# The output products of both feed-forward networks by Strassen's scheme, with the sums of products made in PSUM

## The chip, the cores and the metric

One core of a Trainium2 chip runs the whole kernel. The metric is device time in microseconds (us), shorter is better; three runs of the kernel before gave a median of 3192.24 us. TensorE is called PE, VectorE DVE, ScalarE ACT, GpSimd POOL, and SP is the engine that only issues transfers.

## What is computed

A decoder block: 16 meta tokens are put in front of 1024 tokens, and each of two half-step feed-forward networks (FFN1 before the mixing layers, FFN2 after them) does

```
gate, up = split(rmsnorm(h) @ w_gu, 2)         # 1024 -> 2 x 2816
h = h + 0.5 * (silu(gate) * up) @ w_down       # 2816 -> 1024
```

Between them stand a gated DeltaNet and an RWKV-7 branch, which the change doesn't touch. Everything is float32. The change is to the second product, `@ w_down`, of both networks. Its inner size 2816 is 22 tiles of 128 features, its output 1024 is 8 tiles.

## The kernel before

Features lie on the 128 partitions and tokens along the free axis. A float32 operand x is split into two parts, hi = x rounded to the matmul type, copied by ACT, and lo = x - hi, subtracted by DVE or, where an engine is named, by POOL (`split`). A product then is three matmuls for each tile of inner features: hi by hi, hi by lo, lo by hi (`mm3`, L250 to L260).

`gate_up` (L404) makes silu(gate) * up. It already uses Strassen's scheme in Winograd's form, with 7 products of half-sized quarters instead of 8: the 1040 (FFN1) or 1024 (FFN2) tokens are cut into two halves, the inner features into two halves, the output features into two halves. Its products go to PSUM one by one and DVE adds them up in SBUF (L428). Its results go to DRAM as 22 tiles `hid` (L476).

`down` (L518) is the second product. It takes the 22 tiles of `hid` in four groups of 6, 6, 5 and 5 (`GROUPS`). `Hidden` loads them back (`hr`, three buffers) and splits them (`hd`, eight buffers). Within a group it goes over the 8 output tiles m; for each, `loadw` hands out the weight tile `w` (raw `wraw` by DMA, split by ACT and DVE, one tile ahead), PE makes all matmuls of the group for one chunk of tokens into one PSUM tile `pd`, and DVE adds half of it to the residual `h` (L539). So each weight is split once for a group and used for all tokens, and each `pd` is read once. In the last group the chunks of tokens come one after the other, so that each half of h is done as early as possible: FFN1 then stores it, sums its squares and builds the inputs `uk` of the next stage (`after_block`, L605 to L621); FFN2 makes the final norm and stores the output (L674 to L695). The residual is loaded again from DRAM on POOL's queue when `down` begins (L586, L671). At that point `gate_up` is making its last products and storing the last tiles of `hid`.

A scheduler sets the order of each engine's instructions at build time from the program's data dependences and the buffers of each pool; at run time every engine works through its own list in that order, and an instruction whose inputs or buffer aren't there holds up all behind it on its engine. A tile of a pool with one buffer can be written again only when the last reader of the earlier tile is done.

Of the kernel before, what the change touches and what calls it, by code (L numbers as in the profile page):

```python
# [8 lines left out]
F32 = mybir.dt.float32  # L9
F32R = mybir.dt.float32r  # L10
AF = mybir.ActivationFunctionType
ALU = mybir.AluOpType
# [9 lines left out]
GROUPS = [6, 6, 5, 5]  # L22
# [166 lines left out]
def weight_order():  # L189

    def down_order(n):
        f = 0
        for G in GROUPS:
            for _ in range(2 if f + G == NF else 1):
                for m in range(KD):
                    yield f"wdn{n}", (m, slice(None), slice(f, f + G)), G
            f += G

    def tiles(cts, j=0):
        for ct in cts:  # L200
            yield "win", (ct + j % NJ,), KD

    yield from down_order(1)
    for act, it in schedule():
        yield from tiles(USES.get(act, ()), 0 if act == "segment" else it)
    for _ in range(2):
        for m in range(KD):
            yield "wout", (m,), KD

    yield None  # L210
    yield from down_order(2)
# [51 lines left out]
class Rms:  # L263


    def __init__(self, g, sq, n, add_on=None):
        self.g, self.sq, self.n, self.acc, self.k = g, sq, n, None, 0
        self.eng = add_on or g.nc.vector
# [213 lines left out]
class Hidden:  # L482

    AHEAD = 3

    def __init__(self, g, pool, tot):
        self.g, self.pool, self.tot, self.raws, self.first = g, pool, tot, [], None

    def load(self, f):
        raw = self.pool.tile([P, self.tot], F32, name="hr", tag="hr", bufs=self.AHEAD)  # L490
        self.g.nc.sync.dma_start(raw, self.g.hid[f][:, : self.tot])
        self.raws.append(raw)

    def put(self, hd):
        raw = self.raws.pop(0)
        split(self.g, raw, hd[:, 0, :], hd[:, 1, :])
        return hd

    def ahead(self):
        for f in range(self.AHEAD):  # L500
            self.load(f)
        yield
        yield
        fetchw(self.g)
        yield
        yield
        self.first = self.put(self.pool.tile([P, 2, self.tot], F32R, name="hd0", tag="hd0"))
        yield
        yield


    def tiles(self, sp, f0, G, bufs):
        hid = []
        for f in range(f0, f0 + G):
            if f >= self.AHEAD:
                self.load(f)
            hid.append(self.put(sp.tile([P, 2, self.tot], F32R, name="hd", tag="hd", bufs=bufs)) if f else self.first)
        return hid  # L518


def down(g, sp, hs, which, chunks, hooks, hidden, bufs):

    nc = g.nc
    f0 = 0
    for G in GROUPS:
        hid = hidden.tiles(sp, f0, G, bufs)
        last = f0 + G == NF
        if last:
            hooks.before_last()
        for ci, cs in enumerate([[c] for c in chunks] if last else [chunks]):  # L530
            for m in range(KD):
                wd = loadw(g, f"wdn{which}", m, slice(None), slice(f0, f0 + G))
                for t0, n in cs:
                    pd = mm_tile(g, "pd", n)
                    for c0, cn in halves(n):
                        sl = slice(t0 + c0, t0 + c0 + cn)
                        mm3(g, pd[:, c0 : c0 + cn], wd, G, lambda k: (hid[k][:, 0, sl], hid[k][:, 1, sl]))
                    hv = hs[m][:, t0 : t0 + n]
                    nc.vector.scalar_tensor_tensor(hv, pd, 0.5, hv, op0=ALU.mult, op1=ALU.add)  # L539
                if last:  # L540
                    hooks.after_block(ci, m)
        f0 += G


def ffn1(g):
    tc, nc = g.tc, g.nc
    n = T // 2
    with ExitStack() as ctx:
# [29 lines left out]
        hidden = Hidden(g, ctx.enter_context(tc.tile_pool(name="f1d", bufs=1, reuse_waits="tile")), T)  # L578
# [3 lines left out]
        xctx = ExitStack()  # L582
        sp = ctx.enter_context(tc.tile_pool(name="f1", bufs=1, reuse_waits="tile"))
        hs = [sp.tile([P, T], F32, name=f"h{k}") for k in range(KD)]
        for k in range(KD):
            nc.gpsimd.dma_start(hs[k], g.a["hT"][k])  # L586
        hooks = K()
# [36 lines left out]
        down(g, sp, hs, 1, [c[:2] for c in SEGS], hooks, hidden, 8)  # L624
# [3 lines left out]
def ffn2(g):  # L628
# [3 lines left out]
    with ExitStack() as ctx:  # L632
        right = ExitStack()
        bp = ctx.enter_context(tc.tile_pool(name="f2b", bufs=1, reuse_waits="tile"))
        b = {x: bp.tile([P, HK, 2, n], F32R, name=f"b{x}") for x in ("11", "21")}
# [27 lines left out]
        hidden = Hidden(g, ctx.enter_context(tc.tile_pool(name="f2d", bufs=1, reuse_waits="tile")), SEQ)  # L663
        with tc.tile_pool(name="gs", bufs=1, reuse_waits="tile") as sp:
            gu.send((hidden.ahead(), sp))
        right.close()
        sp = ctx.enter_context(tc.tile_pool(name="f2", bufs=1, reuse_waits="tile"))
        hs = [sp.tile([P, SEQ], F32, name=f"hh{k}") for k in range(KD)]
        for s in range(2):
            for k in range(KD):  # L670
                nc.gpsimd.dma_start(hs[k][:, s * n : (s + 1) * n], g.h3dr[k] if s else g.h2dr[k])  # L671
        hooks = K()
        hooks.before_last = lambda: None
        big = lambda name: sp.tile([P, 4, n], F32, name=name, tag="hd", bufs=8)  # L674
# [23 lines left out]
        down(g, sp, hs, 2, [(0, n), (n, n)], hooks, hidden, 8)  # L698
# [825 lines left out]
```

## Time and profile before

| what | value |
|---|---|
| median of 3 runs | 3192.24 us (3190.23 to 3200.6) |
| the profiled execution's own time | 3192.63 us |
| its span (first to last instruction) | 3190.9 us |
| mean granted TensorE clock | 0.982 |
| PE busy | 3047.0 us, 95% of the span |
| DVE, ACT, POOL busy | 1950.3, 1320.5, 540.7 us |
| FFN1's output product | 497.1 to 761.4 us |
| FFN2's output product | 2925.5 to 3177.4 us |

The profile counts an engine as busy while it has an instruction under way. For PE the ends of matmuls are modelled and overlap, so what counts is how many matmuls start in a stretch. "Idle before, releaser" names what ended an engine's wait. The granted clock is the share of full speed that PE was allowed. Line numbers are those of the kernel before.

### The profile page before, as it was taken

How to read it: one execution, taken by the hardware profiler on the slowest of the kernel's cores; microseconds unless marked ns; L12 is line 12 of the kernel's file. 1: busy time of each engine (PE TensorE's matmuls, PEld its weight loads, DVE VectorE, ACT ScalarE, POOL GpSimd, SP SyncE). 2: the span in 40 equal slices, each digit the busy share in tenths (PEclk: the TensorE clock that was granted, in tenths of full speed). 3: DMA queues.
4: the chain of work that ended last, by engine and by line, in shares of the span. 5: the costliest groups of instructions: out<-in, count | busy, mean ns of one | idle time of the engine just before them, and what ended most of it. 6: DMA issues, size and time to landing. Idle time of an engine off the chain costs nothing. (4 is left out here: it accounts for less than half of the span.)

```text
span 3190.9 us, 57986 instructions
## 1 busy us (share of the span) xinstructions
PE 3047.0 (95%) x23606; PEld 2526.7 (79%) x23606; DVE 1950.3 (61%) x3820; ACT 1320.5 (41%) x2260; POOL 540.7 (17%) x810
## 2 busy tenths in 40 slices
PE   5999999999999999999999999999999899999998
PEld 5999998998877877787776777777776688887886
DVE  7555544346676676676767777777766755555335
ACT  4222222125555545464565455545544422222114
POOL 4222220000011011111111111111101433222000
PEclk8999999999999999999999999999999999999999
DMA  2322224234222222222333232233344232224323
GB/s 93 97 91 80 80 84 160 77 96 141 60 67 75 71 71 58 75 75 69 96 84 78 69 79 72 70 82 76 104 133 172 67 102 86 80 81 149 106 79 111
DMA packets 256554, 286.93 MB, mean 90 GB/s; under 512 B 168272, under 2 KB 174416, under 8 KB 256288
## 3 DMA queue, kind: packets, MB, share of 16 engines
q1 hardware_dynamic: 252048, 271.42, 28.8%
q0 software_dynamic: 2512, 8.65, 0.7%
q8 instruction: 185, 3.03, 0.4%
q10 hardware_dynamic: 1728, 3.16, 0.3%
q14 instruction: 81, 0.66, 0.1%
HBM read 232.70 MB, written 50.47 MB: 89 GB/s over the span
## 5 line engine op out<-in xcount | busy, mean ns | idle before, releaser
L259 PE MATMUL pp<-uk,w 128*128 128x264 f32 (+1 forms) x4824 | 981.0, 353 | 8.1 <-DVE gg L1410 4.5
L259 PEld LDWEIGHTS pp<-uk,w 128*128 128x128 f32 x4824 | 750.3, 192 | 129.7 <-issue 20.3
L154 ACT ACTIVATE w<-wraw 128x1024 fp32r<-128x1024 f32 (+2 forms) x332 | 328.6, 990 | 707.5 <-PE pd L259 288.9
L259 PE MATMUL pd<-hd,w 128*128 128x512 f32 (+1 forms) x2640 | 499.7, 351 | 13.8 <-DVE w L155 6.7
L259 PEld LDWEIGHTS pd<-hd,w 128*128 128x128 f32 x2640 | 428.9, 190 | 83.3 <-DVE w L155 8.6
L422 PE MATMUL pg<-bt,w 128*128 128x260 f32 (+1 forms) x2772 | 457.5, 322 | 22.4 <-ACT bt L154 8.9
L422 PEld LDWEIGHTS pg<-bt,w 128*128 128x128 f32 x2772 | 401.2, 190 | 67.3 <-ACT bt L154 9.6
L428 DVE TENSOR_TENSOR c<-c,pg 128x520 f32<-128x520 f32 (+1 forms) x308 | 208.2, 689 | 368.2 <-PE pg L422 303.4
L155 DVE TENSOR_TENSOR w<-wraw,w 128x1024 fp32r<-128x1024 f32 (+2 forms) x332 | 382.5, 1152 | 63.9 <-ACT w L154 58.4
L422 PE MATMUL pg<-b,w 128*128 128x260 f32 (+1 forms) x2376 | 391.3, 321 | 10.5 <-POOL b L155 5.0
L422 PEld LDWEIGHTS pg<-b,w 128*128 128x128 f32 x2376 | 344.9, 190 | 45.6 <-POOL b L155 5.4
L392 POOL TENSOR_TENSOR wrx<-wrx 128x512 f32<-128x512 f32 x44 | 66.6, 1514 | 575.2 <-DVE w22b L155 305.7
L154 ACT ACTIVATE w<-wrx 128x1024 fp32r<-128x1024 f32 (+1 forms) x66 | 60.2, 912 | 184.9 <-PE pg L422 173.3
L1357 POOL TENSOR_SCALAR sgam<-SBn,gam 128x64 f32<-128x64 f32 x112 | 63.1, 563 | 432.0 <-DVE SBn L1371 400.5
L1230 DVE TENSOR_TENSOR Xb<-Xb,tb 115x126 f32<-115x126 f32 (+22 forms) x496 | 126.7, 255 | 11.3
L1228 DVE TENSOR_TENSOR tb<-Ub,Xb 115x126 f32<-115x126 f32 (+22 forms) x496 | 125.6, 253 | 10.7
L1039 DVE SCALAR_TENSOR_TENSOR acc<-xr,pk,acc 128x528 f32<-128x528 f32 (+1 forms) x144 | 109.0, 757 | 37.5 <-ACT acc L1035 35.0
L539 DVE SCALAR_TENSOR_TENSOR h<-pd,h 128x528 f32<-128x528 f32 (+1 forms) x64 | 44.6, 698 | 119.8 <-PE pd L259 119.8
L539 DVE SCALAR_TENSOR_TENSOR hh<-pd,hh 128x512 f32<-128x512 f32 x64 | 44.2, 690 | 108.4 <-PE pd L259 105.9
L259 PE MATMUL pwo<-uk,w 128*128 128x512 f32 x384 | 104.1, 414 | 5.6 <-DVE w L155 2.1
L1371 DVE SCALAR_TENSOR_TENSOR SBn<-b,gam,sgam 128x64 f32<-128x64 f32 x128 | 36.2, 283 | 94.3 <-PE b L1354 93.9
L835 ACT ACTIVATE sh<-pp,pk 128x528 f32<-128x528 f32 (+1 forms) x54 | 37.3, 691 | 130.7 <-PE pp L259 111.1
(373 smaller groups left out, 4104.9 us busy)
## 6 DMA issues: line engine op xcount, KB each, us to landing
wraw<-in_win SPq DMA_DIRECT2D x150, 512.0 KB, 3.5
wraw<-in_wgu SPq DMA_DIRECT2D x44, 512.0 KB, 3.4
wrx<-in_wgu SPq DMA_DIRECT2D x44, 512.0 KB, 3.5
wraw<-in_wdn SPq DMA_DIRECT2D x48, 320.0 KB, 2.9
wraw<-in_wdn SPq DMA_DIRECT2D x32, 384.0 KB, 3.1
hid<-c SPq DMA_DIRECT2D x44, 260.0 KB, 4.0
hr<-hid SPq DMA_DIRECT2D x22, 520.0 KB, 9.8
hid<-c SPq DMA_DIRECT2D x44, 256.0 KB, 3.1
```

The lines of the kernel that those rows point to most:

```text
L154: g.nc.scalar.activation(hi, src, AF.Copy)
L155: (eng or g.nc.vector).tensor_tensor(lo, src, hi.bitcast(F32), op=ALU.subtract)
L259: g.nc.tensor.matmul(ps, lhsT=l, rhs=r, start=i == 0, stop=i == n - 1)
L392: nc.gpsimd.tensor_tensor(a22, a21, a22, op=ALU.add)
L422: nc.tensor.matmul(ps[:, c0 : c0 + cn], lhsT=l[:, x, k, :], rhs=r[:, k, y, c0 : c0 + cn], start=i == 0, stop=i == 3 * HK - 1)
L428: nc.vector.tensor_tensor(o, x, y, op=ALU.add)
L539: nc.vector.scalar_tensor_tensor(hv, pd, 0.5, hv, op0=ALU.mult, op1=ALU.add)
L835: nc.scalar.activation(sh[:, 1 : 1 + n], ps, AF.Identity, scale=g.V("mu", i))
L1039: nc.vector.scalar_tensor_tensor(acc[:, :n], xr[:, tap : tap + n], V("convw", ct * 4 + tap), acc[:, :n], op0=ALU.mult, op1=ALU.add)
L1228: nc.vector.tensor_tensor(tv, U[:, i, i + 1 :].unsqueeze(2).to_broadcast([npt, nt, ncc]), X[:, i, 0:ncc].unsqueeze(1).to_broadcast([npt, n ...
L1230: nc.vector.tensor_tensor(X[:, i + 1 :, 0:ncc], X[:, i + 1 :, 0:ncc], tv, op=ALU.add)
L1357: nc.gpsimd.tensor_scalar(sg, SB, gam, None, op0=ALU.mult)
```

## The change

The output product takes 18 of the 22 tiles of `hid` by the same scheme of 7 products, in three groups (`NSG`) of six tiles: quarters of three tiles (`GP`) by half of the tokens. The remaining four tiles (`FREST` to `NF`) go as before, chunk after chunk. There are 12 units of work in each network: group by group, and within a group four pairs of output tiles, m and m + 4.

What is added for each unit: two raw weight tiles (`wraw`, `wrc`) and from them six weight forms. "11" and "12" are split as they are (tile `w`). POOL then makes four sums in place in the raw tiles, for the forms "s3" and "s1" (tile `wd31`) and "s2" and "s4" (tile `wd24`). The form "22" (tile `wd22`, the only one with one buffer) is split before those sums, since the first of them writes over a22. What is added for each group: seven forms of the hidden tiles (`down_forms`: 11, t1, t2, 21, t3, 22, t4), again with sums in place, and one buffer for each form. What replaces the sums on DVE: products that share a term are accumulated in the same PSUM tile, with an add to the residual after each step; the three PSUM tiles of a unit are x, y and z, and y gathers four of the seven products.

The program asks for the seven products of a unit in this order, here numbered as they are spoken of below: y1 = 11 by 11, z1 = s1 by t1, y2 = s2 by t2, x = 12 by 21, y3 = s3 by t3, z2 = s4 by 22, y4 = 22 by t4. The first number is the weight form, the second the hidden form. In FFN1 a product is 18 matmuls of 260 columns, in FFN2 9 of 512.

```diff
+GP = 3
+NSG = 3
+FREST = 2 * GP * NSG
...
+def down_weights(g, which, grp, m):
...
+    a = g.wp.tile([P, KD, P], F32, name="wraw", tag="wraw", bufs=2)[:, : 2 * GP]
+    nc.sync.dma_start(a, g.a[f"wdn{which}"][m, :, fs])
+    put(g.wp.tile([P, 2, KD, P], F32R, name="w", tag="w", bufs=WB), a, "11", "12")
+    yield w
+    new = lambda name, k: g.wd.tile([P, 2, k, P], F32R, name=name, tag=name, bufs=2 if k > GP else 1)
+    c = g.wd.tile([P, 2 * GP, P], F32, name="wrc", tag="wrc", bufs=2)
+    nc.sync.dma_start(c, g.a[f"wdn{which}"][m + HK, :, fs])
+    a11, a12, a21, a22 = a[:, :GP], a[:, GP:], c[:, :GP], c[:, GP:]
+    put(new("wd22", GP), a22, "22", eng=nc.gpsimd)
+    nc.gpsimd.tensor_tensor(a22, a21, a22, op=ALU.add)
+    nc.gpsimd.tensor_tensor(a21, a11, a21, op=ALU.subtract)
+    put(new("wd31", 2 * GP), c, "s3", "s1")
+    nc.gpsimd.tensor_tensor(a11, a22, a11, op=ALU.subtract)
+    nc.gpsimd.tensor_tensor(a12, a12, a11, op=ALU.subtract)
+    put(new("wd24", 2 * GP), a, "s2", "s4")
+    yield
...
+def down_forms(g, hidden, grp, place):
...
+    if grp:
+        put("11", b11)
+    else:
+        b["11"] = hidden.b11
+    sums(nc.gpsimd, b11, b12, b11)
+    put("t1", b11)
+    sums(nc.vector, b11, b22, b11)
+    put("t2", b11)
+    put("21", b21, nc.gpsimd)
+    sums(nc.vector, b12, b22, b12)
+    put("t3", b12)
+    put("22", b22, nc.gpsimd)
+    sums(nc.gpsimd, b21, b21, b11)
+    put("t4", b21)
...
+def down(g, hs, which, chunks, hooks, hidden, place, wctx):
...
+    for i, (grp, m) in enumerate(units):
+        l = w
+        if i + 1 < len(units):
+            nxt = down_weights(g, which, *units[i + 1])
+            w = next(nxt)
+            next(nxt)
...
+        x, y, z = (mm_tile(g, name, n) for name in ("pdx", "pdy", "pdz"))
+
+        product(y, l["11"], b["11"], stop=False)
+        add(h11, y)
+        product(z, l["s1"], b["t1"], stop=False)
+        add(h22, z)
+        product(y, l["s2"], b["t2"], False, False)
+        add(h12, y)
+        product(x, l["12"], b["21"])
+        add(h11, x)
+        product(y, l["s3"], b["t3"], False, False)
+        add(h22, y)
+        product(z, l["s4"], b["22"], False)
+        add(h12, z)
+        product(y, l["22"], b["t4"], False)
+        add(h21, y)
+        if m == HK - 1:
+            if grp + 1 < NSG:
+                b = down_forms(g, hidden, grp + 1, place)
...
+    for ci, (t0, n) in enumerate(chunks):
+        for m in range(KD):
+            wd = loadw(g, f"wdn{which}", m, slice(None), slice(FREST, NF))
...
-        for s in range(2):
-            for k in range(KD):
+        for k in (0, 4, 1, 5, 2, 6, 3, 7):
+            for s in range(2):
                 nc.gpsimd.dma_start(hs[k][:, s * n : (s + 1) * n], g.h3dr[k] if s else g.h2dr[k])
```

On PE, in the middle of FFN1's output product: before, the matmuls of one output tile go through the hidden tiles `hd` with one weight tile `w`, three at a time.

```order
L259 MATMUL pd_5070<-hd_4951,w_4966 128x512 x3
L259 MATMUL pd_5070<-hd_4956,w_4966 128x512 x3
L259 MATMUL pd_5070<-hd_4961,w_4966 128x512 x3
L259 MATMUL pd_5095<-hd0_4880,w_5029 128x264 x3
L259 MATMUL pd_5095<-hd_4943,w_5029 128x264 x3
```

Now, on PE, this is one whole unit, the third of FFN1's first group (`hd0`, `ht1`, `h21` and so on are hidden forms, `w`, `wd31`, `wd24`, `wd22` weight forms):

```order
L589 MATMUL pdy_5376<-hd0_4884,w_5201 128x260 x18
L589 MATMUL pdz_5377<-ht1_4980,wd31_5211 128x260 x2
L589 MATMUL pdx_5375<-h21_4997,w_5201 128x260 x6
L589 MATMUL pdy_5376<-ht2_4990,wd24_5216 128x260 x2
L589 MATMUL pdz_5377<-ht1_4980,wd31_5211 128x260 x16
L589 MATMUL pdy_5376<-ht2_4990,wd24_5216 128x260 x16
L589 MATMUL pdx_5375<-h21_4997,w_5201 128x260 x12
L589 MATMUL pdy_5376<-ht3_5007,wd31_5211 128x260 x18
L589 MATMUL pdz_5377<-h22_5014,wd24_5216 128x260 x18
L589 MATMUL pdy_5376<-ht4_5024,wd22_5206 128x260 x18
```

What moved: one weight tile for each output tile has become four for each pair, the second, third and fourth product are broken up and mixed, and `wd22` is read last.

On ACT, at the same place, with what each row waits for: before, one copy for each weight tile.

```order
L154 ACTIVATE w_5218<-wraw_5216 128x768 [waits DMAHW2_49,DVE_49,PE_49]
L154 ACTIVATE w_5281<-wraw_5279 128x768 [waits DMAHW3_49,DVE_49,PE_49]
L154 ACTIVATE w_5344<-wraw_5342 128x768 [waits DMAHW4_49,DVE_49,PE_49]
L154 ACTIVATE w_5407<-wraw_5405 128x768 [waits DMAHW5_49,DVE_49,PE_49]
L154 ACTIVATE hd_5485<-hr_5483 128x1040 [waits DMAHW6_49,PE_49]
```

Now, on ACT, the copies for the unit shown above and the first two of the next one:

```order
L157 ACTIVATE wd22_5206<-wrc_5204 128x384 [waits DMAHW2_49,PE_49,Activation_49]
L157 ACTIVATE wd31_5211<-wrc_5204 128x768 [waits Pool_49]
L157 ACTIVATE wd24_5216<-wraw_5199 128x768 [waits Pool_49]
L157 ACTIVATE w_5513<-wraw_5511 128x768 [waits DMAHW5_49,DVE_49,PE_49]
L157 ACTIVATE wd22_5362<-wrc_5360 128x384 [waits DMAHW2_49,PE_49,Activation_49]
L157 ACTIVATE wd31_5367<-wrc_5360 128x768 [waits DVE_49,Pool_49]
```

What moved: the copies for a unit now wait for POOL, and that into `wd22` for PE. The PE instruction waited for is the last matmul that reads the earlier `wd22`, the last of y4 of the unit before.

On DVE, where FFN1's second group begins (`ht3`, `ht4` are the new group's hidden forms; L555 a sum in place, L582 an add to the residual, `pdy_5761` the y of the new group's first unit):

```order
L555 TENSOR_TENSOR hr_5035<-hr_5041,hr_5035 128x520
L158 TENSOR_TENSOR ht3_5704<-hr_5031,ht3_5704 128x520
L158 TENSOR_TENSOR ht3_5704<-hr_5033,ht3_5704 128x520
L158 TENSOR_TENSOR wd31_5523<-wrc_5516,wd31_5523 128x768
L158 TENSOR_TENSOR ht3_5704<-hr_5035,ht3_5704 128x520
L158 TENSOR_TENSOR wd24_5528<-wraw_5511,wd24_5528 128x768
L158 TENSOR_TENSOR w_5742<-wraw_5740,w_5742 128x768
L158 TENSOR_TENSOR ht4_5721<-hr_5037,ht4_5721 128x520
L158 TENSOR_TENSOR ht4_5721<-hr_5039,ht4_5721 128x520
L158 TENSOR_TENSOR ht4_5721<-hr_5041,ht4_5721 128x520
L582 SCALAR_TENSOR_TENSOR h0_4944<-pdy_5761,h0_4944 128x520
L582 SCALAR_TENSOR_TENSOR h4_4946<-pdz_5762,h4_4946 128x520
```

Before, on DVE between the first two groups (`hd` are the new group's hidden tiles, `h0` its first add):

```order
L539 SCALAR_TENSOR_TENSOR h7_4934<-pd_5410,h7_4934 128x528
L155 TENSOR_TENSOR hd_5485<-hr_5483,hd_5485 128x1040
L155 TENSOR_TENSOR hd_5490<-hr_5488,hd_5490 128x1040
L539 SCALAR_TENSOR_TENSOR h7_4934<-pd_5448,h7_4934 128x512
L155 TENSOR_TENSOR hd_5495<-hr_5493,hd_5495 128x1040
L155 TENSOR_TENSOR w_5500<-wraw_5498,w_5500 128x768
L155 TENSOR_TENSOR hd_6004<-hr_6002,hd_6004 128x1040
L539 SCALAR_TENSOR_TENSOR h0_4927<-pd_5503,h0_4927 128x528
```

What moved: the first add of a new group stands behind all seven forms of that group and three weight splits; before, it stood behind four of the group's splits. On POOL, the loads of the residual (L586 and L671, now issued tile by tile in the order 0, 4, 1, 5, ...) now stand ahead of the splits of `h21` and `h22` and the sums for `ht4` of each network's first unit.

155 lines of the change are left out of this document (96 added, 59 removed).

## The prediction

> **What bounds the kernel now.** The page's first part says that PE is busy nearly all the time. What counts is its pace in the two stretches of the output product, which the table by stage gives, asked for parts well inside them (the first two rows), inside `gate_up` (the third) and for the whole stretches:
>
> ```profile
> PE 3047.0 (95%) x23606; PEld 2526.7 (79%) x23606; DVE 1950.3 (61%) x3820; ACT 1320.5 (41%) x2260; POOL 540.7 (17%) x810
> ```
>
> ```profile
> 530.00:700.00 170.00, 170.00 (x1076) 154.39 (x1076) 60.90 (x74) 27.98 (x32) 0.00 (x0) 1.00 0.26 78
> 2955.00:3140.00 185.00, 185.00 (x818) 153.21 (x817) 75.61 (x95) 39.17 (x48) 0.00 (x0) 1.00 0.28 85
> 100.00:200.00 100.00, 100.00 (x837) 100.00 (x836) 53.19 (x68) 26.85 (x34) 25.79 (x20) 1.00 0.31 100
> 497.10:761.40 264.30, 257.39 (x1591) 232.23 (x1590) 124.21 (x159) 67.76 (x87) 9.14 (x19) 0.98 0.38 125
> 2925.50:3177.40 251.90, 244.50 (x1063) 198.52 (x1062) 118.30 (x148) 66.66 (x83) 11.74 (x18) 1.00 0.37 118
> ```
>
> The columns are the stretch, its length, then busy time and number of instructions of PE, weight load, DVE, ACT and POOL, the granted clock and the transfers. PE never waits in the first three: 0.158 us for a matmul in FFN1's product (two of 264 columns to one of 512), 0.226 us for one of 512 in FFN2's, 0.1195 us for one of 260. DVE, ACT and POOL have time to spare. In the last two rows, the whole stretches, PE's own work is 1584 x 0.158 = 250.3 and 1056 x 0.226 = 238.8 us, so 14.0 and 13.1 us are lost today, most of it at the start. So fewer matmuls are worth their full time, as long as PE goes on without waiting.
>
> **What is saved.** FFN1: 12 units of 126 matmuls of 260 columns, 1512 x 0.1195 = 180.7 us, and the last four tiles with 288 x 0.158 = 45.5; together 226.2, saved 24.1 us. FFN2: 756 + 192 = 948 matmuls of 512, 214.4 us, saved 24.4. In all 48.5 us, if PE never waits more than today.
>
> **The wait in each unit.** By the rows of ACT's order the copy into `wd22` waits for PE's last matmul of the unit before, because `wd22` has one buffer. Behind that copy hangs a chain: POOL's lo of "22", the sum into a22, the difference into a21, ACT's copy into `wd31`, and only then z1, the second product. PE has y1 alone to bridge it. The prices, from the groups by line and from the order of time in `gate_up`, where the same operations stand with 512 columns:
>
> ```profile
> L154 ACT ACTIVATE w<-wraw 128x768 fp32r<-128x768 f32 x16 | 13.5, 846 | 94.0 <-PE pd L259 82.3 <-issue 9.4 <-PE pg L422 2.3
> L154 ACT ACTIVATE w22b<-wrx 128x512 fp32r<-128x512 f32 x11 | 6.8, 619 | 0.9 <-DMA wrx<-in_wgu 0.8
> L393 POOL TENSOR_TENSOR wrx<-wraw,wrx 128x512 f32<-128x512 f32 x19 | 24.4, 1287 | 1.5
> 434.46 1.29 POOL L394 TENSOR_TENSOR wraw<-wrx,wraw 128x512 f32<-128x512 f32 x1
> 435.83 1.29 POOL L395 TENSOR_TENSOR wraw<-wraw 128x512 f32<-128x512 f32 x1
> 437.16 1.06 ACT L154 ACTIVATE w<-wraw 128x1024 fp32r<-128x1024 f32 x1 [7.27 <-POOL wraw L395]
> 462.75 0.64 PE L422 MATMUL pg<-b,w 128*128 128x260 f32 x4
> 462.88 1.06 ACT L154 ACTIVATE w<-wrx 128x1024 fp32r<-128x1024 f32 x1 [4.67 <-PE pg L422]
> ```
>
> Handing over takes 0.13 us from PE to ACT (462.75 to 462.88) and 0.04 between the others (435.83 + 1.29 to 437.16). ACT's copy of 384 columns is 0.50 us by the slope from 512 to 768. POOL's operation of 384 columns is not in the trace; three quarters of 1.29 is 0.97, with something fixed in it 1.0, and one follows the other by 1.07. From the end of y4: 0.13 + 0.50 + 0.04 + (2 x 1.07 + 1.0) + 0.04 + 0.85 = 4.7 us to `wd31`. y1 lasts 18 x 0.1195 = 2.15 us in FFN1 and 9 x 0.226 = 2.04 in FFN2, so PE waits 2.6 and 2.7 us. Then it makes eight matmuls in FFN1 (two of z1, six of x), which ends at 5.7 us, and comes to y2, which needs `wd24`: two more POOL operations, 6.9 us. That is a second wait of 1.2 us. The last unit of a group has another order there and escapes the second one. So an inner unit loses 3.8 us, a group's last 2.6. FFN2 does y1 of each group's second unit early, within the first, so those three find nothing under the chain and lose 4.7 + 1.2 = 5.9.
>
> Counted: FFN1 6 x 3.8 + 3 x 2.6 = 30.6 us; FFN2 3 x 5.9 + 3 x 3.9 + 3 x 2.7 = 37.5.
>
> **What stays covered.** On DVE a unit needs seven adds of 0.69 and three splits of 0.96 us, 7.7 of its 15.1; on ACT 3.1. Adds to the residual now stand between products in the same PSUM tile, but another product of 2 us runs meanwhile; without that cover each of the three for y would cost about 0.8 us. Two weight tiles for a unit are at 0.39 MB each no more than one for 8.5 us today, and the transfers' share is 0.26 to 0.28.
>
> **The change of group.** Each form has one buffer, so the next group's forms can be made only as the last unit gives them free, and all stand in DVE's order ahead of the first add, which y2 waits for. I walk through FFN1, with time 0 at the start of the last unit, which ends at 15.1 + 2.6 = 17.7. These rows give the prices, first without and then with POOL and DVE at work beside each other:
>
> ```profile
> L428 DVE TENSOR_TENSOR c<-c,pg 128x520 f32<-128x520 f32 x138 | 94.0, 694 | 179.9 <-PE pg L422 145.4 <-issue 34.1
> L155 DVE TENSOR_TENSOR w<-wraw,w 128x768 fp32r<-128x768 f32 x16 | 15.3, 958 | 2.3 <-ACT w L154 2.2
> L155 DVE TENSOR_TENSOR bt<-h,bt 128x520 fp32r<-128x520 f32 x16 | 14.2, 919 | 1.8 <-ACT bt L154 1.8
> L366 POOL TENSOR_TENSOR h<-h,h 128x520 f32<-128x520 f32 x4 | 7.3, 1821 | 5.6 <-DVE h L355 5.6
> L353 POOL TENSOR_TENSOR h<-h 128x520 f32<-128x520 f32 x4 | 6.5, 1622 | 1.3 <-DVE h L352 1.3
> ```
>
> x leaves h21's buffer at 11.1, but ACT's first copy into it stands behind a t2 copy that waits for DVE, and is done at 15.3. POOL then makes three splits of 21 and three sums for t4 (6 x 1.31 = 7.9, to 23.2), after them the next unit's `wd22` lo, sum and difference (3.1, to 26.3); ACT's `wd31` comes at 27.2. y1 ended at 19.8: PE waits 7.4 us. On DVE then follow `wd31`, t3, `wd24`, `w` and three splits of t4, and the first add is done at 35.3, where PE has run out at 31.5: 3.8 us more. That is 11.2 us; the same walk for FFN2, with 512 columns and the early y1 to fill, gives 9.0. Four changes of group: 40.4 us. Bounds are 6 us each, if only DVE's 27 operations of 0.69 and 4 of 0.96 us count, and 16 if they run as slowly as the last three rows.
>
> **Start and end.** FFN1's first product loses time today as well, before the hidden tiles are there:
>
> ```profile
> 498.91 1.17 PE L259 MATMUL pd<-hd,w 128*128 128x512 f32 x5 [1.13 <-DVE c L428]
> 502.12 6.07 PE L259 MATMUL pd<-hd,w 128*128 128x264 f32 x28 [2.04 <-DVE w L155]
> 503.42 4.21 POOL L586 DMA_DIRECT2D h<-in_hT  x8 [26.49 <-DMA hid<-c]
> 510.84 0.74 PE L259 MATMUL pd<-hd,w 128*128 128x264 f32 x3 [2.65 <-ACT hd L154]
> ```
>
> In the changed kernel y2 waits for the residual, issued at 503.4, and y4 for six POOL operations behind those eight issues (507.6 + 7.9, then ACT and DVE: 518). Without waits y4 would come at 510.4; so 8 us go, as today: 0. In FFN2 the issues themselves take long:
>
> ```profile
> 2931.65 4.32 POOL L671 DMA_DIRECT2D hh<-h2dr  x8 [25.18 <-DMA hid<-c]
> 2946.37 0.54 POOL L671 DMA_DIRECT2D hh<-h3dr  x1 [0.95 <-DMA hh<-h2dr]
> ```
>
> Nine POOL operations (12 us) now stand behind them, then y4, which could come at 2939.9. With the issues done at 2946.9 that is 2960; with fewer reloads beside them, 2942.5, it is 2955. I take 15 us less the 7 of today: 8, between 2 and 12. At FFN1's end DVE is nearly full, which shorter PE work doesn't help: 2 us.
>
> ```profile
> 735.90:761.40 25.50, 25.50 (x111) 20.65 (x110) 23.65 (x36) 15.35 (x25) 0.39 (x4) 1.00 0.54 176
> ```
>
> **The clock.** Each wait has a second price. In stretches of 3.4 us in which PE is idle for 2.2 us or more, the granted clock is 0.50 right after; with 1.9 it stays (the columns are PE busy, clock, transfers):
>
> ```profile
> 498.36:501.76 3.40, 1.17 (x5) 1.00 0.28 106
> 501.76:505.17 3.41, 3.05 (x10) 0.50 0.88 278
> ...
> 983.02:986.43 3.41, 0.75 (x8) 1.00 0.70 114
> 986.43:993.26 6.83, 6.83 (x67) 0.50 0.41 98
> ...
> 2427.00:2430.40 3.40, 1.54 (x8) 1.00 0.99 355
> 2430.40:2433.80 3.40, 3.17 (x13) 1.00 0.85 310
> 513.90 5.85 PE L259 MATMUL pd<-hd,w 128*128 128x264 f32 x26 [0.56 <-ACT hd L154]
> ```
>
> The last row has 26 matmuls of 264 columns in 5.7 us, 0.22 against 0.12, so a slow stretch costs 45% of itself: 1.55 us for 3.41, and it lasts one or two such stretches. A wait of 2.6, 0.96 of work and a wait of 1.2 put 2.2 idle us into one stretch from 2.8 of 3.41 places at which it can begin, a single 2.6 from 1.6 of them. With 1.5 slow stretches, 2.3 us, that is 1.9 and 1.1 us; of the first some 0.4 are swallowed by the second wait, which slow matmuls shorten. So 1.5 us for 12 inner units and 1.1 for 6 last ones: 25 us. At a change of group the next wait swallows it.
>
> **The sum**, against the profiled execution's own 3192.63 us, which is the median to 0.4 us: -48.5 + 30.6 + 37.5 + 40.4 + 0 + 8 + 2 + 25 = +95, so 3288 us.
>
> **The rivals.** (1) The clock holds. If waits of 2.6 us are still let pass, 25 us fall away: 3263. Against it stand the pairs from 498.36 and 983.02; for it, that the stretches may cut a wait in two. The Trainium skill, TensorE: Matmul & The Clock Gate, "Why this matters for your kernels", asks only for no idle gap over about 3 us, and by that this rival would hold; the trace does not agree, 2.2 us were enough. Chance 0.17. (2) POOL and DVE hinder each other throughout, as in the three slow rows above: 0.4 us more on some 22 POOL operations at each change of group and on three in each of 18 units, 35 + 22 us: 3340 at most. The Trainium skill, SBUF — State Buffer, "Who interferes with whom", says that a DVE instruction with two SBUF inputs and a reading GpSimd one exclude each other for their whole length; that would put a group change at its upper bound. In `gate_up` POOL's 1287 ns speaks against it. Chance 0.11. (3) Faster: the copy into `wd22` is let go before the unit's end, so that POOL's chain runs under the products before. Then the units cost nothing and the clock holds: -48.5 + 24 to 40 + 10, 3178 to 3194. It decides as soon as all waits stay under 48.5 us, 2.0 for each of 24 units. Against it stand the wait for PE in ACT's row and that nothing else can bridge 4.7 us with one product. Chance 0.09.
>
> **The numbers.** The forecast has the remaining 0.63. The lower end takes no clock cost, 6 us for a group change, 2 for FFN2's start and 0.3 less for each chain: 95 - 25 - 16 - 6 - 6, 3235; the upper two slow stretches at each wait (+27), 4 us more for each group change and for FFN2's start (+20): 3335. A difference of 0.3%, 10 us, is about what can be told from none. Faster gets 0.06, the same 0.03, slower 0.91.
>
> **What would show it.** In the changed profile PE should wait about 2.6 us for ACT's `wd31` and 1.2 for `wd24` in nearly every unit, ACT's `wd22` should be ended by PE, and the granted clock should fall to about 0.9 in both stretches, which last some 308 and 304 us. If PE runs through units without those waits, or they are under 2 us on average, the forecast is wrong.

## The result and the profile after

The changed kernel takes 3357.84 us (median of 4 runs, 3354.85 to 3361.3) against 3193.74 of the kernel before beside it (4 runs): the ratio is 1.0512, 95% interval 1.0492 to 1.0533. It is slower by 164 us, where 95 were forecast. The profiled execution's span is 3353.4 us, 162.5 more than before. The table by stage (columns as in the prediction) gives FFN1's and FFN2's output product, what lies between them, and the unit at FFN1's first change of group, all of the changed kernel.

```profile
499.10:848.40 349.30, 261.37 (x1806) 250.66 (x1805) 215.42 (x244) 96.49 (x149) 133.09 (x114) 0.87 0.28 90
3006.80:3339.90 333.10, 255.46 (x955) 191.04 (x953) 197.65 (x230) 95.68 (x145) 132.03 (x111) 0.89 0.26 84
848.40:3006.80 2158.40, 2078.07 (x17223) 1636.03 (x17222) 1445.66 (x3184) 1035.35 (x1886) 381.93 (x665) 0.99 0.29 84
606.90:640.18 33.28, 19.34 (x128) 18.93 (x127) 24.81 (x24) 8.02 (x13) 18.50 (x12) 0.79 0.36 120
```

The two stretches grew by 85.0 and 81.2 us; all else is 3.7 us shorter. Each stretch splits into work (number of matmuls by their time at full pace), idle time (length less PE busy) and a rest, which is half clock and the edges of waits:

| us | before, FFN1 / FFN2 | after | difference | forecast |
|---|---|---|---|---|
| work | 250.3 / 238.8 | 226.2 / 214.4 | -24.1 / -24.4 | -24.1 / -24.4 |
| idle | 6.9 / 7.4 | 87.9 / 77.6 | +81.0 / +70.2 | +53.0 / +63.5 |
| rest | 7.1 / 5.7 | 35.2 / 41.1 | +28.1 / +35.4 | +12.5 / +12.5, and 2 at FFN1's end |

So the saving came as forecast; idle time was forecast 35 us too low, 28 of them in FFN1, and the rest 37 too low. PE's waits (the us in all, how often, the longest):

```profile
PE pdz L589 <- ACT wd L157: 96.3, 24, 9.2
PE pdy L589 <- DVE h L582: 25.5, 5, 12.3
PE pdy L589 <- ACT wd L157: 14.5, 12, 1.6
```

The first row is z1 waiting for `wd31` in all 24 units, the third y2 waiting for `wd24`. The second, FFN1's adds to the residual, was forecast for the changes of group alone; its 12.3 us are the start. The unit chain, in order of time, on PE, ACT, POOL and PE again:

```profile
564.28 2.31 PE L589 MATMUL pdy<-hd,w 128*128 128x260 f32 x18
564.53 0.53 ACT L157 ACTIVATE wd<-wrc 128x384 fp32r<-128x384 f32 x1 [5.63 <-PE pdy L589]
565.13 1.01 POOL L158 TENSOR_TENSOR wd<-wrc,wd 128x384 fp32r<-128x384 f32 x1 [15.90 <-ACT wd L157]
...
568.32 0.84 ACT L157 ACTIVATE wd<-wrc 128x768 fp32r<-128x768 f32 x1 [3.27 <-POOL wrc L533]
569.22 0.50 PE L589 MATMUL pdz<-ht,wd 128*128 128x260 f32 x2 [2.62 <-ACT wd L157]
...
569.44 1.59 POOL L536 TENSOR_TENSOR wraw<-wraw 128x384 f32<-128x384 f32 x1
571.96 0.80 PE L589 MATMUL pdy<-ht,wd 128*128 128x260 f32 x2 [1.53 <-ACT wd L157]
```

The wait of 2.62 is the forecast 2.6. The second is 1.5 and not 1.2, because POOL's last sum took 1.59 us and not 1.0; it runs beside DVE's split of `wd31` (from 569.20 on). And FFN1's start, on DVE, POOL and PE:

```profile
515.73 9.33 DVE L158 TENSOR_TENSOR ht<-hr,ht 128x520 fp32r<-128x520 f32 x3
...
528.30 0.68 DVE L582 SCALAR_TENSOR_TENSOR h<-pdy,h 128x520 f32<-128x520 f32 x1
511.74 4.22 POOL L695 DMA_DIRECT2D h<-in_hT  x8
515.98 3.76 POOL L158 TENSOR_TENSOR h<-hr,h 128x520 fp32r<-128x520 f32 x3
519.70 4.19 POOL L555 TENSOR_TENSOR hr<-hr 128x520 f32<-128x520 f32 x3
...
508.20 0.80 PE L589 MATMUL pdz<-ht,wd 128*128 128x260 f32 x2 [6.78 <-ACT wd L157]
512.66 3.83 PE L589 MATMUL pdz<-ht,wd 128*128 128x260 f32 x16 [3.66 <-DVE wd L158]
...
529.04 4.27 PE L589 MATMUL pdy<-ht,wd 128*128 128x260 f32 x18 [12.32 <-DVE h L582]
```

Three splits, 0.69 us each where POOL is idle, took 9.33 on DVE, nearly all of it while POOL worked (515.98 to 523.89); the first of them alone took 7.03. The add that y2 waits for stands behind them. The DVE row, not the chain, led the experiments. Theory: units pay for the chain behind `wd22`, and in addition POOL's and DVE's operations on SBUF tiles shut each other out, which makes the starts and group changes long. Rival: only the order of DVE's list or the chain counts, and POOL's help is help. Times below are medians, but six variants ran only once (y1 twice, the forms on DVE, both with late forms, the forms of the first group only, and the double buffer with all on DVE but no late forms). The kernel before gave 3188.6 to 3193.7 beside them, with single runs from 3181.9 to 3198.6, so differences of 10 us or less that rest on one run say little.

### The profile page after: what moved, and what is told of

The parts are those of the page before. It is cut to its first block, busy times and chain, and to the rows that moved or that the text cites. A ratio compares the mean times of both kernels' runs of the same rounds, so it can differ in the third digit from the quotient of the medians.

```text
span 3353.4 us, 58903 instructions
## 1 busy us (share of the span) xinstructions
PE 3058.5 (91%) x23714; PEld 2535.6 (76%) x23714; DVE 2138.6 (64%) x4006; ACT 1386.9 (41%) x2398; POOL 798.4 (24%) x1002
## 5 line engine op out<-in xcount | busy, mean ns | idle before, releaser
L157 ACT ACTIVATE w<-wraw 128x1024 fp32r<-128x1024 f32 (+2 forms) x308 | 306.4, 995 | 550.3 <-POOL wraw L395 194.9
L158 DVE TENSOR_TENSOR w<-wraw,w 128x1024 fp32r<-128x1024 f32 (+2 forms) x308 | 361.9, 1175 | 62.5 <-ACT w L157 60.5
L589 PE MATMUL pdy<-ht,wd 128*128 128x260 f32 (+1 forms) x972 | 184.9, 341 | 56.5 <-DVE h L582 25.5
L589 PEld LDWEIGHTS pdy<-ht,wd 128*128 128x128 f32 x972 | 151.7, 203 | 82.9 <-ACT wd L157 19.6
L589 PE MATMUL pdz<-ht,wd 128*128 128x260 f32 (+1 forms) x324 | 88.6, 434 | 104.8 <-ACT wd L157 96.3
L589 PEld LDWEIGHTS pdz<-ht,wd 128*128 128x128 f32 x324 | 69.4, 278 | 120.9 <-ACT wd L157 104.3
L157 ACT ACTIVATE wd<-wrc 128x384 fp32r<-128x384 f32 (+1 forms) x48 | 32.8, 683 | 183.8 <-PE pdy L589 104.2
```

Of the source, the lines that this page charges most:

```text
L157: g.nc.scalar.activation(hi, src, AF.Copy)
L158: (eng or g.nc.vector).tensor_tensor(lo, src, hi.bitcast(F32), op=ALU.subtract)
L589: nc.tensor.matmul(ps[:, c0 : c0 + cn], lhsT=l[:, x, k, :], rhs=r[:, k, y, c0 : c0 + cn], start=start and i == 0, stop=stop and i == 3 * G ...
```

## The experiments

**Two buffers for `wd22`** (one for `wrc`, to make room):

```diff
-    new = ... bufs=2 if k > GP else 1)
-    c = g.wd.tile(... name="wrc", tag="wrc", bufs=2)
+    new = ... bufs=2)
+    c = g.wd.tile(... name="wrc", tag="wrc", bufs=1)
```

> Changed kernel with two buffers for wd22 (and, to make room, one for the raw tile wrc). Chain theory: in the changed kernel an inner unit of FFN1 takes 21.2 us (from 564.28 to 585.49), of which 15.05 is work, 2.6 the wait for wd31, 1.5 that for wd24 and about 2 the half clock behind them. All three hang on the copy into wd22 that waits for the unit's last matmul. With a second buffer POOL's five operations run under the unit before, so an inner unit takes 15.1 to 15.5 us at a granted clock of 1.0. That gives back about 6.6 us in 14 units and some 7 at each of four group changes, about 115 us: 3242, between 3215 and 3270. The waits for the first adds, at both starts and at the group changes, stay, and at the group changes grow from 4.7 to 10 us or more, because DVE's list is as long as before. Rival, POOL and DVE hinder each other in the units themselves: then POOL's five operations, now beside DVE's splits and adds, stretch to 1.5 us and more each, units stay above 18 us, and the time stays above 3290.

Measured: 3287.91 us, 70 less and not 115, above the range. In order of time, PE in an inner unit of FFN1 from 558.56 to 575.09, and at the change of group:

```profile
558.56 2.31 PE L589 MATMUL pdy<-hd,w 128*128 128x260 f32 x18
...
568.52 2.41 PE L589 MATMUL pdy<-ht,wd 128*128 128x260 f32 x18 [1.16 <-DVE h L582]
...
575.09 2.33 PE L589 MATMUL pdy<-hd,w 128*128 128x260 f32 x18
...
618.30 3.77 PE L589 MATMUL pdy<-ht,wd 128*128 128x260 f32 x18 [14.68 <-DVE h L582]
```

PE no longer waits for the chain in FFN1's inner units: 16.5 us for 21.2. What the chain had hidden comes out: 1.16 us for an add that stands behind DVE's split of `wd24`, and 14.7 at each change in FFN1, where I had put "10 us or more". The rival falls for these units: POOL's operations there take 1.01 us, the last 1.61. It doesn't fall everywhere: the last units of FFN1's first two groups take 20.2 and 21.2 us (575.09 to 595.28, 661.61 to 682.78), and FFN2's third unit 19.8 (3024.62 to 3044.43), where y3 waits 3.4 us for an add behind the split of `wd24`.

**y1 twice.**

```diff
         product(y, l["11"], b["11"], stop=False)
+        product(y, l["11"], b["11"], stop=False)
```

> Changed kernel in which every unit's first product y1 is made twice into the same PSUM tile (the second pass starts it anew, so the result stands): 24 x 18 or 9 matmuls more, 50 us more work for PE, put where PE waits for wd31. Without any price of the clock: in 18 units idle time falls from 4.15 to about 1.0 us while 2.15 us of work come in, 17 us less, and at starts and group changes the added work lies inside the waits; 3335 to 3345. If the half clock behind the waits costs 2 to 3 us for each unit, as the difference between 21.2 us and 15.05 + 4.15 says, that goes as well wherever a stretch of 3.4 us no longer holds 2.2 us of idle time: 40 to 50 us more, 3285 to 3305, with a granted clock of 1.0 in the inner units.

Measured: 3346.36 us, 11 less with 50 us more of PE's work, in neither of the two ranges, 1 us above the one without a price of the clock. An inner unit as a row of the table by stage:

```profile
563.20:583.50 20.30, 18.03 (x147) 17.43 (x146) 7.62 (x10) 3.06 (x4) 5.64 (x5) 1.00 0.14 40
```

The total settles nothing, since PE now waits longer for adds behind DVE's weight splits (the products got another order as well). The granted clock rose from 0.87 and 0.89 to 0.92 and 0.93 in the two stretches. In the inner unit shown it is 1.00, and 20.30 is 17.21 of work (144 x 0.1195), 2.27 idle and 0.82 for three waits, so a wait costs 0.27 us beside its idle time in this unit. In the changed kernel the same unit (564.28 to 585.49) has 21.21 - 15.06 - 4.15 = 2.0 left for two waits; 1.5 of it is half clock, as forecast for an inner unit.

**All hidden forms on DVE**, with nothing else changed:

```diff
-    sums(nc.gpsimd, b11, b12, b11)
-    put("21", b21, nc.gpsimd)
+    sums(nc.vector, b11, b12, b11)
+    put("21", b21)
...
```

> Changed kernel in which DVE makes everything for the hidden forms, the lo of 21 and 22 and the sums for t1 and t4 too, which POOL made: 12 operations more on DVE for each group, none on POOL but the weights'. Theory that a subtraction on DVE and an operation on POOL shut each other out: at FFN1's start three splits for t2 took 9.33 us on DVE while POOL worked from 515.98 to 523.89, against 0.62 us each when POOL is idle, so 27 operations on DVE take as long as DVE's and POOL's together. 39 operations of 0.65 us are then 25 us against some 34, the group changes get 5 to 9 us shorter and the starts 5 to 10 us: 35 to 55 us less, 3305 to 3325. Rival, DVE is slow there for a reason of its own (its reads, its own waits for ACT): 12 operations more at 1.3 us make each start and group change up to 15 us longer: 3400 or more.

Measured: 3349.56 us, between both. The groups of FFN1's product, DVE and POOL of the changed kernel, then DVE of this one (busy us, mean ns):

```profile
L158 DVE TENSOR_TENSOR ht<-hr,ht 128x520 fp32r<-128x520 f32 x36 | 48.8, 1389 | 0.3 <-ACT ht L157 0.2
L555 DVE TENSOR_TENSOR hr<-hr 128x520 f32<-128x520 f32 x16 | 19.9, 1264 | 0.0
L158 DVE TENSOR_TENSOR h<-hr,h 128x520 fp32r<-128x520 f32 x6 | 5.6, 958 | 0.0
L158 POOL TENSOR_TENSOR h<-hr,h 128x520 fp32r<-128x520 f32 x18 | 28.7, 1605 | 32.8 <-ACT h L157 32.7
L555 POOL TENSOR_TENSOR hr<-hr 128x520 f32<-128x520 f32 x15 | 23.4, 1573 | 4.8 <-DVE h L158 4.3
```

```profile
L158 DVE TENSOR_TENSOR ht<-hr,ht 128x520 fp32r<-128x520 f32 x36 | 26.5, 781 | 0.9 <-ACT ht L157 0.9
L158 DVE TENSOR_TENSOR h<-hr,h 128x520 fp32r<-128x520 f32 x24 | 20.4, 890 | 0.0
L555 DVE TENSOR_TENSOR hr<-hr 128x520 f32<-128x520 f32 x31 | 20.2, 689 | 0.0
```

DVE alone makes all 91 operations in 67.1 us; in the changed kernel it needed 74.3 for 58 of them, while POOL spent 52.1 on the other 33. So the operations shut each other out, as the theory says, but the time hardly falls: the unit chain stays, and PE waits on for `wd31`.

**Both edits**, the first diff and the third together.

> Both of the edits: two buffers for wd22, and all hidden forms on DVE. If chain and mutual exclusion are two separate causes their gains add up: 115 + 45 us less, 3190 to 3225, which is near the kernel before. If with the chain gone DVE's list is the only bound at the group changes, the second edit counts for more (PE can no longer hide it behind the wait for wd31): 3180 to 3200. If they share one cause the sum is no better than the better one alone, 3240.

Measured: 3278.58 us, 9 under the double buffer alone; the gains didn't add up, and none of the three figures was met. At the change, on DVE, ACT and PE, and the group of one of POOL's weight sums in FFN1's product:

```profile
602.18 0.70 DVE L158 TENSOR_TENSOR ht<-hr,ht 128x520 fp32r<-128x520 f32 x1 [4.42 <-ACT ht L157]
600.78 0.84 ACT L157 ACTIVATE wd<-wrc 128x768 fp32r<-128x768 f32 x1 [7.22 <-POOL wrc L533]
612.43 4.27 PE L589 MATMUL pdy<-ht,wd 128*128 128x260 f32 x18 [14.82 <-DVE h L582]
```

```profile
L535 POOL TENSOR_TENSOR wraw<-wrc,wraw 128x384 f32<-128x384 f32 x12 | 13.6, 1134 | 28.2 <-DVE w L158 27.5
```

DVE waits for ACT, whose list stands at the copy into `wd31`, which waits for POOL; POOL's sums in turn wait for a split on DVE. Weight work left on POOL now holds the others up, and still meets the forms: one of POOL's splits of 384 columns, 1.0 us in an inner unit, takes 4.97 here (from 593.63), beside DVE's splits and sums.

**Late forms**: t3, 22 and t4 are asked for after the first adds of a group's first unit. First with POOL's part as in the double-buffer kernel, then with all forms on DVE.

```diff
+        if m == 0:
+            next(forms)
+            next(forms)
```

> Two buffers for wd22, and the last three hidden forms of a group (t3, 22, t4) asked for only after the first adds of the group's first unit, so that on DVE the first add stands before them and not behind. Order theory: the waits for the first add (14.9 us at FFN1's start, 14.7 at its group changes with two buffers for wd22) come from the adds' place in DVE's list alone; then they shrink to under 3 us and the time falls from 3287.9 by 4 x 12 and 2 x 10 us, to about 3220. Capacity theory: from the start of a group's last unit to the last product of the next unit there are some 28 us, and DVE's 27 operations for forms, POOL's 12, 14 adds and the weights come to over 40 us when DVE and POOL shut each other out; then the waits only move behind the add, to t3, 22 and t4, and the time falls by 10 to 25 us, to 3263 to 3278.

> The same late forms, with all of them on DVE (39 operations of 0.65 us for a group). Capacity theory: 39 x 0.61 + 14 adds x 0.65 + 6 weight splits x 0.9 is 38 us of DVE against 28, plus what POOL's weight sums take: each group change still loses some 12 us, the time is 3250 to 3268, 10 to 25 us under the kernel with these forms on DVE and not late (3278.6). Order theory: 3210.

Measured: 3282.71 and 3262.94 us, 5 and 16 less than without the late forms; the first is a little above its range, and its 5 us can't be told from none. PE's waits for adds from y in FFN1, first and second kernel (56.5 and 49.1 us in all, up to 14.9 and 14.8, without the late forms):

```profile
PE pdy L591 <- DVE h L584: 41.2, 12, 10.1
```

```profile
PE pdy L591 <- DVE h L584: 32.2, 14, 4.7
```

The add's place in the list alone is not it: the waits get shorter and spread. As long as POOL shares the work there is too much of it for both, as the capacity theory had it.

**Forms of the first group only** (the double-buffer kernel, later groups' forms left out):

```diff
-                b = down_forms(g, hidden, grp + 1, place)
+                for f in range(2 * GP * (grp + 1), 2 * GP * (grp + 2)):
+                    hidden.raws.pop(f)
```

> Two buffers for wd22, and the hidden forms of the second and third group left out: all three groups use those of the first, so the forms of 12 of 18 hidden tiles are not made (their tiles are still loaded). Both theories that lay the group change to the forms (order or capacity): from the start of a group's last unit to the start of the next group's second unit the kernel with two buffers needs 53.4 us in FFN1 for 30.1 of work; these 23 us twice and about 20 twice in FFN2 go, 3195 to 3210, and what is left above the kernel before with 48.5 us of work saved, some 55 us, belongs to the two starts and to the waits of 1.2 and 3 us within units. Rival, the change of group is slow because of the residual adds or the weights: then 3260 or more.

Measured: 3221.33 us, 66.6 less, somewhat above the range and far from the rival's 3260: making the forms of a later group, with the waits that follow from it, cost 16.6 us for each of four changes of group.

**Nothing on POOL.** To double buffer, late forms and forms on DVE comes this:

```diff
-    put(new("wd22", GP), a22, "22", eng=nc.gpsimd)
-    nc.gpsimd.tensor_tensor(a22, a21, a22, op=ALU.add)
+    put(new("wd22", GP), a22, "22")
+    nc.vector.tensor_tensor(a22, a21, a22, op=ALU.add)
...
```

> Late forms, two buffers for wd22, and nothing on POOL: forms and weight sums all on DVE. Mutual exclusion theory: POOL's five operations of 1.08 us for a unit become five of some 0.5 on DVE, which nobody hinders, and the two splits of weights no longer stretch beside POOL; DVE has in an inner unit 7 x 0.7 + 3 x 0.96 + 2.5 = 10.3 us of 15.1, so inner units run without waits, and a group change loses 10 to 15 us: 3235 to 3255, the fastest of the variants that do all the work and still slower than the kernel before. Rival, POOL's help counts (two engines get more done than one, even so): slower than the kernel with POOL's weight sums and late forms on DVE by 10 us or more.

Measured: 3188.49 us, against 3192.57 before beside it: ratio 0.9994, 95% interval 0.9979 to 1.0009. Far better than forecast: I had again priced too low what POOL's part costs. An inner unit and both stretches, then two groups of DVE in FFN1's product:

```profile
545.65:560.78 15.13, 15.13 (x129) 15.13 (x127) 9.93 (x15) 3.07 (x4) 0.00 (x0) 1.00 0.18 53
497.65:759.19 261.54, 241.71 (x1806) 232.35 (x1805) 215.85 (x337) 97.62 (x150) 10.08 (x21) 0.95 0.37 121
2929.79:3176.90 247.11, 230.84 (x955) 181.23 (x953) 207.83 (x323) 96.06 (x146) 11.72 (x18) 0.97 0.35 114
```

```profile
L158 DVE TENSOR_TENSOR ht<-hr,ht 128x520 fp32r<-128x520 f32 x36 | 23.3, 691 | 0.0
L532 DVE TENSOR_TENSOR wrc<-wrc 128x384 f32<-128x384 f32 x12 | 6.7, 555 | 0.3
```

In FFN1's product DVE makes 93 operations more than in the changed kernel and is busy no longer (215.85 us for 337, 215.42 for 244). The inner unit has no wait at all. Idle time is 19.8 and 16.3 us, most of it at the starts and the changes of group. The two stretches together are 7.6 us shorter than before; what lies between them takes 2170.6 us for 2164.1, which no run explains.

**Which of the edits it was**: all of POOL's arithmetic to DVE and nothing else (the diff of the forms on DVE and the one just shown); then that with the double buffer, without the late forms.

> Only this is changed in the changed kernel: what POOL computes in the output product (lo of 21 and 22, sums for t1 and t4, lo of wd22, four weight sums) is computed by DVE. wd22 keeps its one buffer, the forms are not late. Mutual exclusion theory: the chain behind wd22 becomes 0.13 + 0.50 + 0.04 + 2 x 0.48 + 0.55 + 0.04 + 0.85 = 3.1 us against y1's 2.15, so PE waits 1.0 us for wd31 and not at all for wd24, the clock holds, and 18 units cost 22 us in place of about 110; at the group changes DVE's list is longer, but no operation of it is stretched, and the wait for wd31 of 9.2 us goes. 3235 to 3265. Rival, only the double buffer and the late forms gave the gain of the last variant (3188.5) and moving POOL's work matters little by itself, as when the forms alone were moved (3349.6): 3320 or more.

> All on DVE and two buffers for wd22, but the forms not late: against the variant with all three edits (3188.5) this shows what the place of the first add in DVE's list is worth once POOL is out of the way. At each group change 39 operations of 0.61 us and the weights stand before the first add, 24 + 7 us from the second of the last unit's products on, which PE meets some 8 us too early; at FFN1's start as well: 5 x 8 us more, 3215 to 3240. If the list's order does not matter without POOL: 3188 to 3195.

Measured: 3261.29 (ratio to before 1.0228, 1.0184 to 1.0272) and 3218.5 us, both as the theory had them. An inner unit's one wait in the first, and what PE waited for `wd31` in all, 96.3 before:

```profile
552.91 0.50 PE L589 MATMUL pdz<-ht,wd 128*128 128x260 f32 x2 [1.17 <-ACT wd L157]
```

```profile
PE pdz L589 <- ACT wd L157: 48.3, 24, 5.5
```

The edits in this order are worth 96.5, 42.8 and 30 us. With POOL out of the chain the single buffer still costs 1.2 us of idle time in an inner unit.

**Useless work for POOL** in the variant with all edits:

```diff
+        for _ in range(7):
+            nc.gpsimd.tensor_tensor(busy, l["22"][:, 0, :2, :].bitcast(F32), busy, op=ALU.subtract)
```

> The variant with all three edits (3188.5 us), with work for POOL that nobody needs: in each unit seven subtractions of 256 columns, of wd22 and a small tile of its own, about 5 us of POOL in a unit of 15 us. No other engine waits for them but the copy into the buffer of wd22 after next. Mutual exclusion theory: DVE's subtractions between two SBUF tiles stand still while one of these runs, some of them take 1.3 to 2 us for 0.55 to 0.95, and waits of PE come back, most at the starts and group changes where DVE is full: 3205 to 3250. Rival, engines work side by side without harm and POOL's earlier price was only its slow chain: 3188, within 5 us, with DVE's subtractions as before.

Measured: 3229.25 us, 41 more (ratio to before 1.0127, 1.0084 to 1.0171). The group of one of DVE's weight sums, then DVE, PE and POOL in an inner unit and POOL at a change of group:

```profile
L532 DVE TENSOR_TENSOR wrc<-wrc 128x384 f32<-128x384 f32 x12 | 10.5, 878 | 0.3
```

```profile
553.54 0.98 DVE L532 TENSOR_TENSOR wrc<-wrc 128x384 f32<-128x384 f32 x1
...
561.92 2.42 PE L591 MATMUL pdy<-ht,wd 128*128 128x260 f32 x18 [1.05 <-DVE h L584]
...
553.05 7.39 POOL L613 TENSOR_TENSOR busy<-wd,busy 128x256 f32<-128x256 f32 x7 [6.84 <-ACT wd L157]
...
591.26 18.74 POOL L613 TENSOR_TENSOR busy<-wd,busy 128x256 f32<-128x256 f32 x5 [14.06 <-ACT wd L157]
```

Work that hardly anyone waits for makes DVE's sum take 0.98 us for 0.55, and where DVE has a full list POOL needs 3.7 us for each of five operations that take 1.06 in the inner unit. It works both ways. The adds of PSUM to the residual stay at 0.69 us throughout. The new waits are not mostly at the starts and changes, where I had put them: of the 14.4 us that PE idles more in FFN1, 10.3 are eight waits of 1.0 to 2.1 us in units that had none. At the starts PE's wait for `wd31` grows by 3.7 and 3.4 us; there POOL also issues the residual's loads later, behind the useless work (508.07 for 503.73 in FFN1, 2946.10 for 2935.85 in FFN2), and that isn't exclusion.

**x second in a group's first unit**, of the variant with all edits:

```diff
+        if m == 0:
+            product(x, l["12"], b["21"])
+            add(h11, x)
         product(z, l["s1"], b["t1"], stop=False)
```

> The variant with all three edits (two buffers for wd22, all on DVE, late forms: 3188.5 us, the kernel before 3192.6 in the same runs) in which the first unit of each group makes x = 12 by 21 as its second product, ahead of z1, and the form 21 is made ahead of t1. What is left there is 18 us lost at FFN1's start, some 10 at FFN2's, and 8 at each group change; at the start PE waits 5.8 us for wd31 with DVE's list of eight operations ahead of it, while x needs only three splits. Capacity theory: DVE's work stays the same, so the gain is only what PE can do meanwhile, 2 to 3 us at each start and 0 to 1 at a group change, and with them perhaps a slow stretch of the clock: 3178 to 3186, a ratio to the kernel before of 0.996 to 0.999. Rival, the form 21 ahead of t1 delays z1 by as much as x gains: 3188 or more.

Measured: 3193.64 us, ratio to before 1.0002 (0.9992 to 1.0012): no gain, as the rival had it. PE at FFN1's start:

```profile
502.07 0.62 PE L591 MATMUL pdx<-h,w 128*128 128x260 f32 x3 [2.17 <-DVE h L158]
...
519.14 4.18 PE L591 MATMUL pdy<-ht,wd 128*128 128x260 f32 x18 [8.68 <-DVE h L584]
```

The wait of 5.8 us became 2.2, and one of 8.7 for the first add took its place.

## Why the prediction came out too low

Of the 69 us that the forecast lacks, 37 are the rest, which is mostly the clock, and 35 idle time, less 4 elsewhere. Of the idle time 16 us are FFN1's start, 7 the unit's chain in FFN1, 5 FFN1's changes of group and 7 FFN2.

**The saving** of 48.5 us is there, and the variant without waits shows PE at 15.13 us a unit. **The unit's chain** is right in its mechanism and to 0.1 us in its first wait, 2.62 for 2.6, with some luck: from the end of y4 to z1 it took 4.94 us (564.28 to 569.22) and not 4.7, as ACT began 0.25 us behind PE and not 0.13, while the profile counts y1 as busy for 2.31 and not 2.15. The price was 6.8 us too low in FFN1 (37.4 idle for 30.6), for the second wait (1.5 for 1.2) and because "The last unit of a group has another order there and escapes the second one" did not hold in two of FFN1's three groups: 1.0 us for `wd24` and 1.9 for an add behind the new forms.

**The step that failed** is "so 8 us go, as today: 0" for FFN1's start. PE idled there for 6.78 + 3.66 + 12.32 = 22.8 us, 16 more than before. I had counted the loads of the residual and POOL's six operations behind them. The first two waits are z1's, for `wd31`, whose sums stand in POOL's list between splits of a hidden form and whose lo stands in DVE's list behind such splits; the prediction has no wait for z1 there. The third is y2's: DVE's whole list of forms stands ahead of the first add, with DVE busy for 30.3 of 33.9 us. Nor was the residual "issued at 503.4": in FFN1 its loads stand ahead of only the second three of POOL's six splits, and eight POOL operations put them off to 511.74. At the changes of group I had seen DVE's list, and priced its operations at 0.69 us and POOL's at 1.31; beside each other POOL's took 1.6 to 1.8 and DVE's up to 1.9, so 13.9 us and not 11.2. FFN2's start, 11.5 us idle where all of FFN2's stretch had 7.4 before, was within its bounds.

**The second rival was no rival but part of the case.** "POOL and DVE hinder each other" was priced as 0.4 us on POOL's operations; even so its sum, 3288 + 57 = 3345 (the text has 3340), stays under the measured time. It is DVE that loses more, up to 6.3 us on one operation (7.03 for 0.69). "In `gate_up` POOL's 1287 ns speaks against it" was no evidence, since a duration says nothing as long as one doesn't look for what ran beside it: from 431.73 to 437.12, where POOL's four operations took 1.29 us each, DVE ran only adds from PSUM, one of them:

```profile
434.18 0.69 DVE L428 TENSOR_TENSOR c<-c,pg 128x520 f32<-128x520 f32 x1 [1.92 <-PE pg L422]
```

The Trainium skill, SBUF — State Buffer, "Who interferes with whom", says that a DVE instruction with two SBUF inputs and a reading GpSimd one exclude each other, and that one with at most one SBUF input is spared; these runs agree on both (1389 ns against 781, 0.69 us for the adds either way). Moving POOL's arithmetic was worth 96.5 us; some of that is the shorter chain. With the double buffer, where PE doesn't wait for the chain in FFN1's inner units, it was still worth 69 us (3287.91 to 3218.5), and 94 with late forms as well (3282.71 to 3188.49). The runs don't divide it further. Of the 41 us that 168 useless POOL operations cost, the new waits within units show the exclusion by itself; what the later loads at the starts, and a copy that waits for these operations, add isn't measured.

**The clock** is the term that was mis-sized most: 25 us, with "the next wait swallows it" at a group change, and 2 at FFN1's end, where the rest measured 63.5. Two inner units of the changed kernel, PE in order of time:

```profile
645.14 0.51 PE L589 MATMUL pdz<-ht,wd 128*128 128x260 f32 x2 [2.63 <-ACT wd L157]
645.49 0.88 PE L589 MATMUL pdx<-h,w 128*128 128x260 f32 x6
...
667.50 0.80 PE L589 MATMUL pdz<-ht,wd 128*128 128x260 f32 x2 [2.61 <-ACT wd L157]
668.10 1.50 PE L589 MATMUL pdx<-h,w 128*128 128x260 f32 x6
```

After the same wait six matmuls take 0.88 us in one and 1.50 in the other. That it hangs on how the stretches cut the wait is the prediction's reading; no run varied it. Some units pay 1.5 us, others more, and the unit at a change of group has 33.28 - 15.06 - 13.94 = 4.3 us of rest, since slow matmuls came after its last wait too. The prediction also had no price for the edges of a wait. PE waited 66 times in the two stretches, 11 times before; at 0.27 us the 55 more are 15 us, which leaves some 49 of the 63.5 for half clock. That is an estimate, as 0.27 was measured in one unit of FFN1. The first rival (the clock holds) fell: 0.87 and 0.89 were granted, and a wait of 2.6 us was enough. The Trainium skill, TensorE: Matmul & The Clock Gate, "Why this matters for your kernels", lets gaps of up to about 3 us pass; the runs do not agree. The third rival (`wd22` let go early) did not happen either: ACT's copy into it was ended by PE.

## What to carry to other kernels

Before giving arithmetic to the engine that has time to spare, look what it reads: two engines that shut each other out are one engine, and the faster one should have the work. A chain across three engines behind a buffer with one copy is priced from the end of its last reader, and where it ends, what stands behind in the lists of the engines comes next. Even the best variant turned 48.5 us saved on the bounding engine into no difference that can be told: idle time in the two stretches, most of it at starts and changes of group, rose by 22 us, the rest (half clock and edges) by 19, and the remaining 7.6 were lost between the stretches.

## What the runs showed of the hardware

- A subtraction on DVE with two SBUF inputs (128x520, 0.69 us) took 3.1 us on average of three, and 7.03 once, beside a row of POOL operations; a POOL operation took 3.7 us on average of five, for 1.1, beside a row of DVE's. An add from PSUM with one SBUF input took 0.69 us either way.
- In one unit with matmuls of 260 columns a wait cost PE 0.27 us more than the idle time that the profile gives it. Some of that lies at the modelled end of the last matmul: 18 in a row count as busy for 2.31 us where their pace makes 2.15.
- After one wait of 2.6 us in a unit of 21 six matmuls took 1.50 us, after another 0.88: such a wait can halve the clock (0.58 was granted from 666.80 to 670.20, 0.50 from there to 673.60). Over FFN1's 349 us, 0.87 of full speed was granted.
